# Output projections of a two-layer backbone on one Trainium2 core: each weight tile loaded and split for every chunk of columns, or once

## The chip, the cores and the metric

One core of a Trainium2 chip runs the whole program in one launch. The metric is device time in microseconds, the median of several executions; lower is better. All data are float32 in memory.

## The reference, cut to what matters

```python
# layer 0: two mixers side by side, one output projection (1024 -> 1024), for 256 context and 1024 latent tokens
y = jnp.concatenate([y_a, y_b], axis=-1) @ w_out       # ab_mixer: y_a gMLP half, y_b gated DeltaNet half
lat = lat + g1 * y_lat;  cx = cx + cg1 * y_ctx
lat = lat + g2 * conv_ffn(modulate(rms_norm(lat, norm2_g), sh2, sc2), w_up, conv_w, w_down)   # cx alike

# layer 1: latent attention, 8 heads of 128, 1024 latent tokens only
y_lat = block_attention(qn_l, qr_l, kn, kr, v) @ w_out  # (1024, 1024) @ (1024, 1024)
lat = lat + g1 * y_lat
lat = lat + g2 * conv_ffn(modulate(rms_norm(lat, norm2_g), sh2, sc2), w_up, conv_w, w_down)
```

## The kernel before

Activations lie in SBUF with features on the 128 partitions and tokens along the free side. `xa` holds the residual stream: 8 tiles of 128 features by 1280 tokens in layer 0 (256 context tokens first), by 1024 tokens in layer 1.

Every float32 product is made of three matmuls. `split` writes a float32 tile as two tiles of TensorE's fp32r type, a high part (a cast, L126 on POOL or L124 on ACT) and a low part (the difference, L133, on DVE; on POOL too where the engine is called "pools"). `mm3` then gives, for each tile of 128 input features, high x high (L140), high weight x low activation (L141) and low weight x high activation (L142). `weights` (L144) loads a raw weight tile `wur` through SP's DMA queue and splits it into `wuh` and `wul`; `stream` hands out such tiles by number, made on first use. The pool has 3 buffers for the raw tile and 2 each for the parts.

**Layer 0's second half.** The projection's input has two halves of 512 features. The second (`ybh`, `ybl`, from the DeltaNet scan's `o`) comes last. It is done in three chunks of tokens: 512 to 1023 (512 columns), 256 to 511 and 1024 to 1279 (256 columns each). For each chunk, `out0` (L1474) runs over 8 output tiles `ot`, each with 4 weight tiles of 128 x 128 in one 256 KB load, 12 matmuls, and one addition into `xa` on DVE (L1488). Since the chunks are the outer loop, the stream has 24 loads and 24 splits (of 128 x 512 each). Woven into the chunks are the RMS norms of the chunks before (sums `nsum`, `nall` on PE; `nm`, L229, L230 and six L266 on DVE with L264, L267 on ACT and L263 on POOL for the scaling) and the first operands of the ConvFFN, `B11` and `B21` (high part on POOL or ACT, low part on DVE). The scan's end stands directly ahead: `gdn_out` normalises the last two token tiles of `o` (L1468 to L1472; temporaries `osq`, `osr`, `osm`, `osg`), after which the last `ybh`, `ybl` are split.

**Layer 1.** `out1` (L1768) takes the attention output `o`, splits it into `oh` (ACT) and `ol` (DVE), and does three chunks of 512, 256 and 256 tokens (`END`) over 8 output tiles each, with 8 weight tiles of 128 x 128 in one 512 KB load, 24 matmuls and one addition (L1800). That makes 24 loads and 24 splits of 128 x 1024; the first three are "pools". The norms of the chunks before stand between them as in layer 0.

Behind each of the two stages comes the ConvFFN, whose first matmuls are `upa` (L408 to L410) on `B11`.

A framework with tile pools and a scheduler sets the order on each engine; every engine then works its list in order, and SP issues all loads and stores in one list. PSUM has 8 banks, 7 of them under one tag (`bank`, L118) for accumulators. Pool `hc` (and in layer 1 its counterpart) has "rooms", pairs of 128 x 2048 tiles that the ConvFFN's operands take: `room("B11", ...)` and so on. SBUF that a pool takes over from one that was released is guarded by the last users of the old tiles.

Of the kernel before, what the change touches and what calls it, by code (L numbers as in the profile page):

```python
# [7 lines left out]
F32 = mybir.dt.float32  # L8
# [7 lines left out]
P = 128  # L16
D = 1024
KD = D // P
# [17 lines left out]
END = [(0, 512), (512, 256), (768, 256)]  # L36
# [31 lines left out]
def weave(main, fill, n=1, rest=True):  # L68

    for _ in main:  # L70
        for _ in range(n):
            next(fill, None)
    if rest:
        drain(fill)
# [23 lines left out]
class Kern:  # L98
# [55 lines left out]
    def stream(self, pool, srcs, shape, tag, eng, bufs_raw=2, bufs=2, n=None):  # L154

        made = {}

        def get(i):
            if i not in made and i < len(srcs):
                made[i] = self.weights(pool, srcs[i], shape, tag, eng if isinstance(eng, str) else eng(i), bufs_raw, bufs, n)  # L160
            return made.get(i)
        return get
# [1605 lines left out]
    def out1(self, wp, op, o, xa, xd, g1, norm, ready):  # L1768


        nc, tc, I = self.nc, self.tc, self.I
        with ExitStack() as es:
            yp = es.enter_context(tc.tile_pool(name="y1", bufs=1))
            np_ = es.enter_context(tc.tile_pool(name="n2", bufs=1))
            get = self.stream(wp, [I["w_out1"][ot] for ot in range(KD)] * len(END), [P, KD, P], "wu",
                              lambda i: "pools" if i < 3 else "pool", 3)
            get(0)
            get(1)
            yh = yp.tile([P, KD, SEQ], F32R, name="oh")
# [9 lines left out]
            pend, i = iter(()), 0  # L1789
# [22 lines left out]
    def run(self):  # L1812
        nc, tc, I = self.nc, self.tc, self.I
        with ExitStack() as es:
# [54 lines left out]
            g1, sh2, gs2, g2 = self.modv(0, 2), self.modv(0, 3), self.gains(0, 4, ng[:, 1]), self.modv(0, 5)  # L1869
            xap = tc.alloc_tile_pool(name="xa", bufs=1)  # L1870
            xa = xap.tile([P, KD, NT], F32, name="xa")
            op = tc.alloc_tile_pool(name="yb", bufs=1)
            o = op.tile([P, NH, NC, P], F32, name="o")
# [26 lines left out]
            w_half1 = [I["w_out0"][1, ot] for ot in range(KD)]  # L1900
            next(scan)
            with ExitStack() as es2:
                yp = es2.enter_context(tc.tile_pool(name="y0a", bufs=1, side="right"))
                wp = es2.enter_context(tc.tile_pool(name="wo0a", bufs=2, side="right"))
                get = self.stream(wp, w_half1, [P, 4, P], "wo", "pool", 3)
                get(0)
                y = half1(yp, 0, CTX, 0)
# [5 lines left out]
            keep = lambda c0, cn: nc.sync.dma_start(dr["xs"][:, :, c0:c0 + cn], xa[:, :, c0:c0 + cn])  # L1913

            def norm(tmp, c0, cn, steps=True):
                r = 1 if c0 < CTX else 0
                return self.mod_x(tmp, [xv(k, c0, cn) for k in range(KD)], cn, gs2[:, r, :], sh2[:, r, :], steps)
            ffw = tc.alloc_tile_pool(name="ffw", bufs=2, side="right")
# [18 lines left out]
            with ExitStack() as es2:  # L1937
                yp = es2.enter_context(tc.tile_pool(name="y0b", bufs=1))
                np_ = es2.enter_context(tc.tile_pool(name="n0b", bufs=1))
                tmps = self.temps(np_, nsq=5, nr=1, nt=0, width=256)  # L1940
                get = self.stream(ffw, w_half1 * 3, [P, KD, P], "wu", "pool", 3, n=4)
                y = [half1(yp, 512, 512, 0), half1(yp, 256, 256, 1)]
                keep(0, CTX)
                weave(self.out0(get, [y[0]], xa, g1), norm(tmps, 0, CTX), 2)
                keep(512, 512)
                y.append(half1(yp, 1024, 256, 0))
                weave(self.out0(lambda i: get(KD + i), [y[1]], xa, g1), norm(tmps, 512, 256), 2)
                keep(256, 256)
                weave(self.out0(lambda i: get(2 * KD + i), [y[2]], xa, g1),
                      chain(norm(tmps, 768, 256), context(), firsts(), norm(tmps, 256, 256)), 3)  # L1950
                keep(1024, 256)
            op.release()
# [36 lines left out]
            h = {}  # L1989
# [207 lines left out]
```

## Time and profile before

| | us |
|---|---|
| median of 3 runs | 3290.85 (3288.29 to 3294.72) |
| profiled execution, whole | 3285.33 |
| its span in the profile | 3283.5 |
| PE busy | 3116.2 (95%) |
| DVE busy | 2180.9 (66%) |
| POOL busy | 1340.1 (41%) |
| ACT busy | 1105.7 (34%) |

The span is the time from the first to the last instruction of the core in the profiled execution. An engine's busy time is the sum over its instructions; the mean granted TensorE clock over the span was 0.978 of full speed. Times of single instructions are counted from the start of the span.

### The profile page before, as it was taken

The page shows a single profiled execution, that of the slowest core. Times are in us where ns is not written, and L with a number is a line of the kernel's source. Part 1 is how long each engine was busy: PE and PEld are TensorE (multiplying, and loading weights), DVE is VectorE, ACT ScalarE, POOL GpSimd, SP SyncE. Part 2 cuts the span into 40 slices and gives each one's busy share as a digit, 9 for nine tenths or more (in the row PEclk, how much of TensorE's full clock was granted, in tenths as well). Part 3 has the DMA queues.
Part 4 walks back from the last instruction along what each step waited for, and adds up shares of the span by engine and source line. Part 5 has one row for each costly group of instructions (what it writes and reads, how often), then busy time and mean ns, then how long its engine had stood idle before and what let it go on. Part 6 is the DMA issues. An engine that isn't in the chain of part 4 may idle for free. (4 is left out here: it accounts for less than half of the span.)

```text
span 3283.5 us, 48865 instructions
## 1 busy us (share of the span) xinstructions
PE 3116.2 (95%) x19029; PEld 2604.8 (79%) x19029; DVE 2180.9 (66%) x3245; ACT 1105.7 (34%) x2136; POOL 1340.1 (41%) x1210
## 2 busy tenths in 40 slices
PE   7999899998899999998999999999998899999998
PEld 5677777886677788886889778888987677778888
DVE  6332876567776678873487455666656788889355
ACT  5322233333333333340021245555542333333110
POOL 3234323654444354442355222222134566665243
PEclk9999999999899999999999999999999899999999
DMA  7344946753335421244457322000034122224554
GB/s 252 122 148 129 302 135 210 235 157 112 97 121 165 157 89 71 69 159 145 142 192 233 93 80 72 27 22 22 8 116 148 58 78 84 83 78 168 194 194 150
DMA packets 257959, 419.82 MB, mean 128 GB/s; under 512 B 47024, under 2 KB 163968, under 8 KB 257600
## 3 DMA queue, kind: packets, MB, share of 16 engines
q1 hardware_dynamic: 257728, 416.70, 39.6%
q8 instruction: 150, 2.46, 0.3%
q14 instruction: 81, 0.66, 0.1%
HBM read 335.85 MB, written 80.78 MB: 127 GB/s over the span
## 5 line engine op out<-in xcount | busy, mean ns | idle before, releaser
L632 PE MATMUL dn<-ah,wdh 128*128 128x256 f32 (+1 forms) x1232 | 391.1, 319 | 15.0 <-POOL wdh L126 12.9
L634 PE MATMUL dn<-ah,wdl 128*128 128x256 f32 (+1 forms) x1232 | 385.5, 319 | 11.2 <-DVE wdl L133 11.1
L633 PE MATMUL dn<-al,wdh 128*128 128x256 f32 (+1 forms) x1232 | 388.7, 317 | 0.0
L126 POOL TENSOR_SCALAR wdh<-wdr 128x1024 fp32r<-128x1024 f32 x154 | 192.1, 1249 | 345.7 <-PE dn L633 222.2
L133 DVE TENSOR_TENSOR wdl<-wdr,wdh 128x1024 fp32r<-128x1024 f32 x154 | 200.2, 1304 | 191.2 <-POOL wdh L126 187.6
L126 POOL TENSOR_SCALAR wuh<-wur 128x1024 fp32r<-128x1024 f32 (+1 forms) x142 | 171.0, 1205 | 270.1 <-PE upc L409 95.8
L632 PEld LDWEIGHTS dn<-ah,wdh 128*128 128x128 f32 x1232 | 237.4, 193 | 37.2 <-POOL wdh L126 13.9
L133 DVE TENSOR_TENSOR wul<-wur,wuh 128x1024 fp32r<-128x1024 f32 (+1 forms) x139 | 199.2, 1434 | 97.0 <-POOL wuh L126 96.6
L634 PEld LDWEIGHTS dn<-ah,wdl 128*128 128x128 f32 x1232 | 234.9, 193 | 30.3 <-DVE wdl L133 13.8
L633 PEld LDWEIGHTS dn<-al,wdh 128*128 128x128 f32 x1232 | 237.0, 192 | 15.3
L1719 POOL TENSOR_SCALAR p<-p,rsm 128x1280 f32<-128x1280 f32 x63 | 84.8, 1345 | 325.3 <-DVE rsm L1712 167.4
L674 DVE SCALAR_TENSOR_TENSOR y<-raw,fconv,y 128x1023 f32<-128x1023 f32 (+1 forms) x132 | 171.1, 1324 | 35.2 <-ACT y L420 34.9
L676 DVE SCALAR_TENSOR_TENSOR y<-raw,fconv,y 128x1023 f32<-128x1023 f32 (+1 forms) x132 | 187.6, 1443 | 0.1
L140 PE MATMUL proj<-hh,wih 128*128 128x512 f32 (+1 forms) x512 | 183.1, 359 | 0.0
L142 PE MATMUL proj<-hh,wil 128*128 128x512 f32 (+1 forms) x512 | 176.4, 345 | 1.0 <-DVE wil L133 1.0
L141 PE MATMUL proj<-hl,wih 128*128 128x512 f32 (+1 forms) x512 | 177.0, 346 | 0.1
L427 POOL TENSOR_TENSOR y<-y,y 128x1280 f32<-128x1280 f32 (+1 forms) x44 | 128.0, 2910 | 105.0 <-issue 58.4
L393 POOL TENSOR_TENSOR s<-wur 128x512 f32<-128x512 f32 x42 | 72.4, 1723 | 191.9 <-DMA wur<-in_w_up 140.8
L1701 DVE TENSOR_REDUCE mx<-sc 128x1 f32<-128x512 f32 (+1 forms) x192 | 114.6, 597 | 40.2 <-PE sc L1700 38.0
L420 ACT ACTIVATE y<-raw,fconv 128x1280 f32<-128x1280 f32 (+1 forms) x88 | 110.8, 1260 | 83.0 <-DVE raw L436 81.1
L111 ACT ACTIVATE p<-sc,nmx 128x512 f32<-128x512 f32 (+1 forms) x192 | 116.2, 617 | 49.1 <-DVE nmx L1705 48.9
L133 DVE TENSOR_TENSOR pl<-pt,ph 128x512 fp32r<-128x512 f32 (+1 forms) x192 | 108.8, 593 | 8.1 <-ACT ph L124 7.5
(535 smaller groups left out, 9268.2 us busy)
## 6 DMA issues: line engine op xcount, KB each, us to landing
wdr<-in_w_down SPq DMA_DIRECT2D x154, 512.0 KB, 3.8
adaw<-in_ada_w SPq DMA_DIRECT2D x96, 512.0 KB, 4.1
wur<-in_w_up SPq DMA_DIRECT2D x88, 512.0 KB, 3.6
al<-act SPq DMA_DIRECT2D x20, 1024.0 KB, 7.4
t<-t SPq DMA_DIRECT2D x20, 768.0 KB, 6.4
act<-y SPq DMA_DIRECT2D x22, 640.0 KB, 3.0
wur<-in_w_out SPq DMA_DIRECT2D x24, 512.0 KB, 3.5
act<-y SPq DMA_DIRECT2D x22, 512.0 KB, 2.6
```

The source lines that it names most:

```text
L111: self.nc.scalar.activation(out, in_, func, **kw)
L126: nc.gpsimd.tensor_scalar(dst, src, 1.0, 0.0, op0=ALU.mult, op1=ALU.add)
L133: (self.nc.gpsimd if eng == "pools" else self.nc.vector).tensor_tensor(lo, src, f(hi), ALU.subtract)
L140: nc.tensor.matmul(ps, wh, xh, start=first and i == 0, stop=False)
L141: nc.tensor.matmul(ps, wh, xl, start=False, stop=False)
L142: nc.tensor.matmul(ps, wl, xh, start=False, stop=last and i == n - 1)
L427: nc.gpsimd.tensor_tensor(y[1], y[0], y[1], ALU.mult)
L632: nc.tensor.matmul(pss[o], wh[:, q, :], ah, start=pr == j == 0, stop=False)
L633: nc.tensor.matmul(pss[o], wh[:, q, :], al, start=False, stop=False)
L634: nc.tensor.matmul(pss[o], wl[:, q, :], ah, start=False, stop=pr == npr - 1 and j == 1)
L674: nc.vector.scalar_tensor_tensor(out=y[:, s0 + 1:e], in0=raw[:, s0:e - 1], scalar=w[:, 0:1], in1=y[:, s0 + 1:e], op0=ALU.mult, op1=ALU.add)
L676: nc.vector.scalar_tensor_tensor(out=y[:, s0:e - 1], in0=raw[:, s0 + 1:e], scalar=w[:, 2:3], in1=y[:, s0:e - 1], op0=ALU.mult, op1=ALU.add)
```

## The change

In layer 0, the eight weight tiles of the second half are loaded as four pairs of 512 KB, each split once, into the rooms `T1` (pairs 0 and 1) and `B22` (pairs 2 and 3); all three chunks read them there. 24 loads and splits of 128 x 512 become 4 of 128 x 1024. In layer 1, output tiles 0 to 3 are loaded and split once, "pools" (high and low part on POOL), into rooms `B11` and `B21`; tiles 4 to 7 are streamed for each chunk as before, and the kept tiles 0 and 1 of the later chunks ask for tiles 4 and 5 ahead of time. 24 loads and splits become 16. In each layer the kept parts are called `wkh` and `wkl`; their rooms are taken by the ConvFFN's operands afterwards.

```diff
@@ out1
-            get = self.stream(wp, [I["w_out1"][ot] for ot in range(KD)] * len(END), [P, KD, P], "wu",
-                              lambda i: "pools" if i < 3 else "pool", 3)
+            keep = [t for r in ("B11", "B21") for t in zip(*[(h[:, 0:2], h[:, 2:4]) for h in self.room(r, "wk")])]
+            keep = [[t.rearrange("p a (b f) -> p (a b) f", f=P) for t in hl] for hl in keep]
+            srcs = [I["w_out1"][ot] for ot in range(4, KD)] * len(END)
+            stream = self.stream(wp, srcs, [P, KD, P], "wu", "pool", 3, 2)
+            made = set()
+
+            def get(i):
+                c, ot = divmod(i, KD)
+                if c == len(END):
+                    return None
+                if ot >= 4:
+                    return stream(4 * c + ot - 4)
+                if c == 0 and ot not in made:
+                    made.add(ot)
+                    raw = wp.tile([P, KD, P], F32, tag="wur", name="wur", bufs=3)
+                    nc.sync.dma_start(raw, I["w_out1"][ot])
+                    self.split(*keep[ot], raw, "pools")
+                if c and ot < 2:
+                    stream(4 * c + ot)
+                return keep[ot]
             get(0)
             get(1)
@@ run
-                get = self.stream(ffw, w_half1 * 3, [P, KD, P], "wu", "pool", 3, n=4)
+                made = {}
+
+                def get(i):
+
+                    i = i % KD
+                    if i // 2 not in made:
+                        j = i // 2
+                        raw = ffw.tile([P, KD, P], F32, tag="wur", name="wur", bufs=3)
+                        nc.sync.dma_start(raw.rearrange("p (o k) f -> p o k f", o=2),
+                                          I["w_out0"][1, 2 * j:2 * j + 2].rearrange("o p k f -> p o k f"))
+                        if j % 2 == 0:
+                            made["room"] = [t.rearrange("p a (b f) -> p (a b) f", f=P) for t in self.room(("T1", "B22")[j // 2], "wk")]
+                        made[j] = [t[:, 8 * (j % 2):8 * (j % 2) + 8] for t in made["room"]]
+                        self.split(*made[j], raw, "pool")
+                    return tuple(t[:, 4 * (i % 2):4 * (i % 2) + 4] for t in made[i // 2])
                 y = [half1(yp, 512, 512, 0), half1(yp, 256, 256, 1)]
                 keep(0, CTX)
                 weave(self.out0(get, [y[0]], xa, g1), norm(tmps, 0, CTX), 2)
                 keep(512, 512)
                 y.append(half1(yp, 1024, 256, 0))
-                weave(self.out0(lambda i: get(KD + i), [y[1]], xa, g1), norm(tmps, 512, 256), 2)
+                weave(self.out0(get, [y[1]], xa, g1), norm(tmps, 512, 256), 2)
                 keep(256, 256)
-                weave(self.out0(lambda i: get(2 * KD + i), [y[2]], xa, g1),
+                weave(self.out0(get, [y[2]], xa, g1),
                       chain(norm(tmps, 768, 256), context(), firsts(), norm(tmps, 256, 256)), 3)
```

What this does to the lists of the engines is to be seen in three places.

The first is POOL at the end of layer 0's scan. Before (`o<-o,osg` are the scan's last two products, `wuh` the weights' casts):

```order
L126 TENSOR_SCALAR wuh_7390<-wur_7388 128x512
L126 TENSOR_SCALAR wuh_7409<-wur_7407 128x512
L1472 TENSOR_TENSOR o_4541<-o_4541,osg_7162 128x4x128
L126 TENSOR_SCALAR wuh_7434<-wur_7432 128x512
L1472 TENSOR_TENSOR o_4541<-o_4541,osg_7166 128x4x128
L126 TENSOR_SCALAR wuh_7458<-wur_7456 128x512
L206 TENSOR_TENSOR nsq_7469<-xa_4537 128x256
L126 TENSOR_SCALAR wuh_7486<-wur_7484 128x512
```

And with the change (`wkh_7390` is room T1, `wkh_7472` room B22):

```order
L1472 TENSOR_TENSOR o_4541<-o_4541,osg_7162 128x4x128
L1472 TENSOR_TENSOR o_4541<-o_4541,osg_7166 128x4x128
L126 TENSOR_SCALAR wkh_7390<-wur_7388 128x1024
L126 TENSOR_SCALAR wkh_7390<-wur_7426 128x1024
L126 TENSOR_SCALAR wkh_7472<-wur_7470 128x1024
L206 TENSOR_TENSOR nsq_7455<-xa_4537 128x256
L126 TENSOR_SCALAR wkh_7472<-wur_7541 128x1024
```

The first cast of the projection's weights now stands behind the scan's last product, since room T1 lies where the scan's temporaries lay; four casts of 128 x 1024 are all there are, and the list goes on with the ConvFFN's weights.

The second is DVE at the same place. Before (L229 to L1471 are the scan's last normalisation; `wul` the weights' low parts):

```order
L1471 TENSOR_TENSOR o_4541<-o_4541,osr_7323 128x4x128
L133 TENSOR_TENSOR wul_7391<-wur_7388,wuh_7390 128x512
L133 TENSOR_TENSOR wul_7410<-wur_7407,wuh_7409 128x512
L229 SCALAR_TENSOR_TENSOR osq_7165<-osq_7165,osm_7336 128x512
L230 SCALAR_TENSOR_TENSOR osr_7335<-osq_7165,osr_7335 128x512
L1471 TENSOR_TENSOR o_4541<-o_4541,osr_7335 128x4x128
L1488 SCALAR_TENSOR_TENSOR xa_4537<-wo_7394,mv02_4526,xa_4537 128x512
L133 TENSOR_TENSOR wul_7435<-wur_7432,wuh_7434 128x512
```

And with the change:

```order
L229 SCALAR_TENSOR_TENSOR osq_7165<-osq_7165,osm_7336 128x512
L230 SCALAR_TENSOR_TENSOR osr_7335<-osq_7165,osr_7335 128x512
L1471 TENSOR_TENSOR o_4541<-o_4541,osr_7335 128x4x128
L133 TENSOR_TENSOR ybl256_7378<-o_4541,ybh256_7377 128x256 x3
L133 TENSOR_TENSOR wkl_7391<-wur_7388,wkh_7390 128x1024
L133 TENSOR_TENSOR ybl256_7378<-o_4541,ybh256_7377 128x256
L133 TENSOR_TENSOR wkl_7391<-wur_7426,wkh_7390 128x1024
L133 TENSOR_TENSOR wkl_7473<-wur_7470,wkh_7472 128x1024
L133 TENSOR_TENSOR wkl_7473<-wur_7541,wkh_7472 128x1024
L133 TENSOR_TENSOR wul_8004<-wur_7999,wuh_8003 128x1024
L1488 SCALAR_TENSOR_TENSOR xa_4537<-wo_7394,mv02_4526,xa_4537 128x512
```

The two low parts that stood inside the scan's last normalisation are gone; the first `wkl` stands behind it and behind three low parts of `ybl256`. All four `wkl`, and the first low part for the ConvFFN (`wul_8004`), stand ahead of the first addition L1488. On PE, the L140 and L141 of three output tiles now stand ahead of the first L142, where those of two did.

The third is POOL at the end of layer 1's attention. Before (`p` is the last softmax product):

```order
L126 TENSOR_SCALAR wuh_22776<-wur_22774 128x1024
L1717 TENSOR_SCALAR p_22640<-p_22640,rsm_22645 128x256
L133 TENSOR_TENSOR wul_22777<-wur_22774,wuh_22776 128x1024
L126 TENSOR_SCALAR wuh_22782<-wur_22780 128x1024
L133 TENSOR_TENSOR wul_22783<-wur_22780,wuh_22782 128x1024
L126 TENSOR_SCALAR wuh_22899<-wur_22897 128x1024
L133 TENSOR_TENSOR wul_22900<-wur_22897,wuh_22899 128x1024
```

And with the change (`wkh_22650` is room B11, `wkh_22652` room B21):

```order
L1717 TENSOR_SCALAR p_22516<-p_22516,rsm_22521 128x256
L126 TENSOR_SCALAR wkh_22650<-wur_22654 128x1024
L126 TENSOR_SCALAR wkh_22650<-wur_22658 128x1024
L126 TENSOR_SCALAR wkh_22652<-wur_22773 128x1024
L133 TENSOR_TENSOR wkl_22651<-wur_22654,wkh_22650 128x1024
L133 TENSOR_TENSOR wkl_22651<-wur_22658,wkh_22650 128x1024
L133 TENSOR_TENSOR wkl_22653<-wur_22773,wkh_22652 128x1024
L126 TENSOR_SCALAR wkh_22652<-wur_22803 128x1024
L133 TENSOR_TENSOR wkl_22653<-wur_22803,wkh_22652 128x1024
```

The first cast stood ahead of the last softmax product and now stands behind it; each low part followed its cast, and now three casts go ahead of the first low part, and four low parts instead of three are POOL's. Room B11 is also guarded by PE's last attention matmul (L142), which read what lay there. Here too the L140 and L141 of three output tiles now stand ahead of PE's first L142, instead of two L140 and one L141.

## Rows read from the trace of the kernel before

**Rows 1.** The page, costliest groups of instructions: splits into hi and lo.
```profile
L126 POOL TENSOR_SCALAR wuh<-wur 128x1024 fp32r<-128x1024 f32 (+1 forms) x142 | 171.0, 1205 | 270.1 <-PE upc L409 95.8
...
L133 DVE TENSOR_TENSOR wul<-wur,wuh 128x1024 fp32r<-128x1024 f32 (+1 forms) x139 | 199.2, 1434 | 97.0 <-POOL wuh L126 96.6
```

**Rows 2.** Waits of PE, 745 to 870 us: total us, times, longest us.
```profile
PE wo L140 <- POOL wuh L126: 8.2, 9, 3.9
PE wo L142 <- DVE wul L133: 5.9, 4, 2.4
```

**Rows 3.** Waits of PE, 2420 to 2570 us.
```profile
PE wo L142 <- DVE wul L133: 5.6, 2, 3.9
PE wo L140 <- POOL wuh L126: 4.6, 4, 1.5
PE wo L142 <- POOL wul L133: 1.7, 1, 1.7
```

**Rows 4.** Windows: length, PE, PEld, DVE, ACT, POOL busy (xcount), PEclk, DMA share, GB/s.
```profile
766.00:775.00 9.00, 5.08 (x17) 3.68 (x16) 7.57 (x10) 3.12 (x5) 3.34 (x3) 0.81 0.76 243
775.00:785.00 10.00, 10.00 (x50) 6.84 (x50) 6.96 (x11) 2.06 (x6) 4.22 (x5) 1.00 0.27 80
812.00:824.00 12.00, 7.31 (x50) 6.49 (x50) 10.14 (x19) 7.25 (x16) 6.47 (x7) 0.95 0.30 87
824.00:844.00 20.00, 16.23 (x117) 12.80 (x117) 17.45 (x27) 8.81 (x20) 10.78 (x13) 0.93 0.56 170
2497.00:2512.00 15.00, 8.76 (x63) 7.72 (x62) 15.00 (x14) 8.67 (x13) 11.16 (x7) 0.78 0.29 94
2530.00:2545.00 15.00, 11.84 (x84) 11.38 (x83) 12.32 (x16) 3.91 (x9) 5.09 (x6) 0.89 0.34 107
2560.00:2620.00 60.00, 44.82 (x227) 37.51 (x226) 45.37 (x45) 18.86 (x28) 28.46 (x17) 0.86 0.12 36
```

**Rows 5.** PE timeline, layer 0: start us, duration us, instruction, idle before.
```profile
766.25 0.28 PE L142 MATMUL wo<-ybh,wol 128*128 128x256 f32 x1
770.45 0.51 PE L140 MATMUL wo<-ybh,wuh 128*128 128x512 f32 x1 [3.92 <-POOL wuh L126]
...
771.63 0.73 PE L142 MATMUL wo<-ybh,wul 128*128 128x512 f32 x1
...
846.82 0.99 PE L408 MATMUL upa<-B11h,wuh 128*128 128x512 f32 x1
```

**Rows 6.** POOL timeline, layer 0.
```profile
769.32 1.66 POOL L126 TENSOR_SCALAR wuh<-wur 128x512 fp32r<-128x512 f32 x2 [6.78 <-DMA wur<-in_w_out]
...
776.14 1.29 POOL L1472 TENSOR_TENSOR o<-o,osg 128x512 f32<-128x512 f32 x1
```

**Rows 7.** ACT timeline, layer 0.
```profile
770.75 0.63 ACT L228 ACTIVATE osq<-osr 128x512 f32<-128x512 f32 x1
```

**Rows 8.** DVE timeline, layer 0.
```profile
770.43 2.78 DVE L133 TENSOR_TENSOR wul<-wur,wuh 128x512 fp32r<-128x512 f32 x2 [0.51 <-POOL wuh L126]
773.13 0.68 DVE L229 SCALAR_TENSOR_TENSOR osq<-osq,osm 128x512 f32<-128x512 f32 x1
...
779.67 1.50 DVE L133 TENSOR_TENSOR ybl<-o,ybh 128x256 fp32r<-128x256 f32 x3
...
835.48 5.69 DVE L266 SCALAR_TENSOR_TENSOR xa<-xa,gs,nr 128x256 f32<-128x256 f32 x6
```

**Rows 9.** POOL timeline, layer 1.
```profile
2420.00 1.05 POOL L126 TENSOR_SCALAR wuh<-wur 128x1024 fp32r<-128x1024 f32 x1 [2.65 <-ACT ph L124]
...
2421.47 2.39 POOL L133 TENSOR_TENSOR wul<-wur,wuh 128x1024 fp32r<-128x1024 f32 x1
```

**Rows 10.** PE timeline, layer 1.
```profile
2427.29 0.73 PE L140 MATMUL wo<-oh,wuh 128*128 128x512 f32 x2 [0.99 <-ACT oh L124]
...
2428.35 0.40 PE L142 MATMUL wo<-oh,wul 128*128 128x512 f32 x1
```

**Rows 11.** DVE timeline, layer 1.
```profile
2498.36 9.26 DVE L266 SCALAR_TENSOR_TENSOR xa<-xa,gs,t 128x512 f32<-128x512 f32 x6
```

## The prediction

> **What bounds the kernel now.** I began with the shares of busy time: PE 95%, everything else at 66% or less. So the kernel is TensorE's, and a change to two short stages can only be worth what PE loses in them. The chain that ended last says the same in its shares and gives no place; I therefore went to the waits of PE over each of the two stages.
>
> In layer 0's stage PE waited 8.2 us for high parts of the projection's weights, in 9 waits of which the longest took 3.9, and 5.9 us for low parts, in 4 waits [rows 2]. In layer 1's stage it waited 5.6 us for low parts from DVE, 4.6 for high parts, and 1.7 for one low part that POOL made [rows 3]. Together 26.0 us out of 3283.5. The reader should see that these are all waits on splits of weights, that is, on the work which the change cuts from 24 to 4 and from 24 to 16 splits.
>
> Then the windows, to see what else goes with the waits. Over 766 to 775 us PE was busy 5.1 of 9 us and the granted clock was 0.81; 775 to 785 is full and at full clock, 50 instructions in 10 us; in 812 to 844 PE was busy 7.3 of 12 and 16.2 of 20 us at 0.95 and 0.93 of full clock; in layer 1 the bad stretches are 2497 to 2512 (8.8 of 15 us, clock 0.78) and 2530 to 2545 (11.8 of 15, 0.89) [rows 4]. [...]
>
> Last, the timelines at both starts, because the lists of the engines show that the first split moves there.
>
> **Layer 0, what is removed.** All waits but the first: 8.2 - 3.9 + 5.9 = 10.2 us. After the first chunk all weights are there, so no cast can be late. The 20 splits that go took some 0.8 us each on POOL [rows 6] and up to 1.4 on DVE [rows 8]; neither engine's own time is on the path, apart from the waits counted. The clock: a granted 0.95 over 12 us and 0.93 over 20 us is half speed for 2 x 0.05 x 12 + 2 x 0.07 x 20 = 4.0 us, in which half the work is undone: 2.0 us back. The loads cost nothing either way: over 775 to 785 the DMA engines were busy 0.27 of the time [rows 4].
>
> **Layer 0, what is moved: a late start.** PE's last matmul of the stage before is at 766.25, and the first one on the new weights at 770.45, with the first L142 at 771.63 [rows 5]. POOL made the first two casts at 769.32, ahead of the scan's last product at 776.14 [rows 6]. With the change the cast stands behind that product. How early can the product come? ACT's L228 before it ended at 770.75 + 0.63 = 771.4 [rows 7]. DVE then has L229, L230 and L1471; L229 ran at 773.13 since two low parts took DVE from 770.43 for 2.78 us [rows 8], and these are gone. So three operations of 0.7 us from 771.4: 773.5. The product, 1.29 us [rows 6]: 774.8. The cast of 128 x 1024, 1.2 us on average [rows 1]: 776.0, and the first L140 at 776.1. The first low part stands on DVE behind three `ybl` (1.50 us [rows 8]), which need ACT's cast of the product and end at about 776.8; then 1.43 us [rows 1]: the first L142 at 778.3, which is 6.7 us later than at 771.63. In that hole PE does what it did later before: two more matmuls of 512 columns and some five sums of the norm, 1.5 us. Net loss 5.2 us. Bounds: 3 us if the product follows faster and DVE takes the low part first, 8 if the cast and low part take the time that they take beside another busy engine (the two low parts of half the size took 1.4 us each at 770.43).
>
> Layer 0 in sum: 10.2 + 2.0 - 5.2 = 7.0 us.
>
> **Layer 0, what is late next.** The stage's end is the first `upa` at 846.82 [rows 5], and it needs `B11`, whose low part comes after six L266 of 5.69 us at 835.48 on DVE [rows 8]. DVE loses 20 of 24 low parts, and this norm can start earlier as the chunk before it ends earlier; I let it move with the chunk, and put the case where it doesn't among the rivals.
>
> **Layer 1, what is removed.** The 1.7 us wait falls on an output tile that is now kept, and its low part is made some 5 us before PE comes to it. Of the other 10.2 us, half of the splits in the second and third chunk stay (8 of 16). A kept tile between two streamed ones gives the streams twice the time, so I expect more than half back; but the 3.9 us wait is for a low part which stands on DVE behind six L266 of 512 columns, 9.26 us at 2498.36 [rows 11], and those stay. I take two thirds: 6.8 us (bounds 3 and 10.2). The clock: half speed for 2 x 0.22 x 15 + 2 x 0.11 x 15 = 9.9 us, 5.0 us of work; two thirds of that is 3.3.
>
> **Layer 1, what is moved.** POOL made the first high part at 2420.00 and its low part at 2421.47 (2.39 us) [rows 9], during the attention. In the new order the first cast waits for PE's last attention matmul, since room B11 lies where that reads. PE sat 0.99 us ahead of 2427.29 [rows 10], so that matmul ended at 2426.3. Three casts of 1.05 us and one low part of 2.39: 2431.9. PE's first L142 comes at 2432.0 instead of 2428.35 [rows 10], 3.65 us late; three more matmuls of 0.23 us are done in the hole. Net loss 3.0 us. From there POOL makes a low part every 2.4 us, while PE needs 5.5 us for the 24 matmuls of one output tile, so it isn't overtaken again. Bounds: 1 and 6 us.
>
> Layer 1 in sum: 1.7 + 6.8 + 3.3 - 3.0 = 8.8 us.
>
> [...] After the 3.9 us wait at 770.45 PE ran at a granted 0.81 until 775, which is half speed for 2 x 0.19 x 9 = 3.4 us and 1.7 us of work [rows 4, 5]. [...] In layer 0 that stretch is in the time of before already. [...]
>
> **The rest.** [...]
>
> Sum: 7.0 + 8.8 + 2.0 = 17.8, say 18 us. Against the profiled execution's 3285.33 that gives 3267; the median of the runs is 5.5 us above that execution, so the forecast is 3290.85 - 18 = 3273 us.
>
> **Rivals.**
>
> A, the forecast: both stages gain as summed, 12 to 24 us. For it speaks that the waits are named and that the order shows them gone.
>
> B, the norms set the pace: six L266 of 5.69 and 9.26 us on DVE [rows 8, 11], with the low part of B11 behind, end as late as before apart from a few us, and PE waits for `nsum`, `npt` or B11 instead of weights. Then each layer keeps some 4 us: 8, 3283 us. DVE had only 2.5 of 20 us free in 824 to 844 [rows 4], which speaks for it; against it, eight or nine low parts were in that stretch, and these go.
>
> C, more: all of layer 1's 10.2 and 5.0 us come back and the hole of layer 0 is half as long: 18 + 5 + 2.6, about 26 us, 3265 us.
>
> D, the other side: on DVE the first addition L1488 stands behind the ConvFFN's first low part, and that behind its load. A raw buffer comes free for this load when the second `wkl` is done, at about 780; with load, cast and low part the addition follows at about 787. PE can fill six accumulators (the norm holds one of seven) of 12 matmuls, 2.8 us each, so it stops at about 795. There are 8 us to spare; the change loses only if that load lands 26 us later than I think, and by over 0.2% from 33 us on. Nothing in a DMA share of 0.27 at that time speaks for it; but loads stand in one list behind stores of `xa`, and I haven't seen it run.
>
> E, it is given back: behind layer 1's stage PE was busy 44.8 of 60 us, at clock 0.86 [rows 4]. If what it waits for there, and behind layer 0's stage, doesn't come earlier, the gain becomes a longer wait there: 3291 us. Against it: these waits hang on the norm of the last chunk, which moves with the stage.
>
> **Chances and numbers.** A 0.55, B 0.20, C 0.10, E 0.08, D 0.07. A change of under 0.2%, 6.6 us, can't be told from none here. Faster by more than that: A, C and three quarters of B, 0.80; within: the rest of B and E, 0.13; slower: D, 0.07. The range of 8 in 10, from C's 3265 less the error of its bounds to the worst end of B: 3260 to 3286.
>
> **What would show it.** In the changed kernel's profile: the first L142 on kept weights about 6.7 us after 771.63 and about 3.7 us after 2428.35; no waits of PE for weights in layer 0 behind the first; at most 4 us of them in layer 1's later chunks; full clock in the last chunk of layer 0; the first `upa` at about 839 in layer 0, and layer 1's 9 us before its old place relative to that. Wrong would make it: a first L142 after 785 in layer 0, additions later than 795, or a new wait of PE for B11 as long as the ones that went.

## The result and the profile after

| | before | changed |
|---|---|---|
| median, us | 3291.55 (4 runs, 3288.29 to 3294.72) | 3270.93 (4 runs, 3268.68 to 3274.09) |
| profiled execution, us | 3285.33 | 3269.30 |
| its span, us | 3283.5 | 3267.2 |
| PE, DVE, POOL, ACT busy, us | 3116.2, 2180.9, 1340.1, 1105.7 | 3102.1, 2166.1, 1321.0, 1103.7 |

The ratio of the times is 0.9944, with a 95% interval from 0.9932 to 0.9956: 20.6 us less by the medians, 16.3 by the two spans. The forecast was 3273 us and 18 us less.

The waits of PE in layer 0's stage, to be held against [rows 2]:

```profile
PE wo L140 <- POOL wkh L126: 9.6, 1, 9.6
PE nall L217 <- DVE npt L214: 2.8, 4, 1.0
...
PE nsum L196 <- POOL nsq L206: 0.7, 1, 0.7
```

And in layer 1's, against [rows 3]:

```profile
PE wo L140 <- POOL wkh L126: 2.4, 3, 1.3
PE wo L142 <- DVE wul L133: 2.3, 2, 1.5
PE wo L142 <- POOL wkl L133: 1.5, 1, 1.5
...
PE upa L408 <- POOL wuh L126: 0.9, 1, 0.9
PE wo L141 <- DVE ol L133: 0.8, 1, 0.8
```

In layer 0 one wait for the projection's new weights is left, the first, and it grew from 3.9 to 9.6 us. The wait for the norm's sums, which DVE copies (`npt`) before PE's `nall` can read them, grew from 0.6 to 2.8 us. In layer 1, the 11.9 us for weights of the projection became 6.2, of which 3.9 (`wkh`, `wkl`) are at the start; `upa` and `ol` are new with 1.7 us.

The windows (length, busy time and instructions of PE, PEld, DVE, ACT and POOL, granted clock, DMA share, GB/s) of the same two stages, against [rows 4]:

```profile
775.00:780.00 5.00, 2.80 (x6) 1.82 (x6) 3.51 (x4) 1.33 (x4) 4.41 (x4) 0.50 0.40 148
...
785.00:805.00 20.00, 19.39 (x89) 15.07 (x88) 13.58 (x21) 6.05 (x15) 6.04 (x6) 1.00 0.37 123
805.00:824.00 19.00, 18.38 (x158) 16.54 (x156) 14.53 (x28) 10.73 (x27) 4.73 (x6) 1.00 0.30 111
824.00:839.00 15.00, 12.68 (x91) 9.35 (x90) 12.47 (x21) 8.67 (x19) 4.33 (x5) 1.00 0.28 97
...
2418.00:2444.00 26.00, 21.24 (x80) 15.68 (x79) 24.25 (x26) 9.61 (x26) 18.25 (x10) 0.87 0.71 243
...
2485.00:2505.00 20.00, 19.13 (x158) 17.91 (x158) 15.31 (x17) 9.00 (x15) 8.42 (x7) 1.00 0.12 34
2505.00:2521.00 16.00, 16.00 (x132) 14.86 (x130) 12.90 (x18) 3.57 (x6) 5.66 (x5) 1.00 0.51 158
2521.00:2537.00 16.00, 13.61 (x80) 10.48 (x79) 15.45 (x16) 7.58 (x15) 10.81 (x9) 1.00 0.60 193
```

From 785 us to the end of layer 0's stage the clock is full, where it was 0.93 to 0.95 from 812 to 844; in layer 1 the place of the 0.78 and the 0.89 is at full clock too. At both starts a stretch runs at half clock. In layer 0 that is not new: the 0.50 over 775 to 780 stands in the place of the 0.81 over 766 to 775 [rows 4]. In layer 1 it is: 0.87 on average over 2418 to 2444, with 0.50 in each us from 2423 to 2429, where the same window of before, with the stage's start in it, has 1.00:

```profile
2418.00:2444.00 26.00, 21.55 (x113) 17.20 (x112) 17.05 (x36) 15.38 (x39) 12.01 (x8) 1.00 0.77 273
```

PE's rows of layer 0, against [rows 5]: the last matmul of the stage before, the first two of the new weights, the change to 256 columns, and `upa`:

```profile
767.36 0.28 PE L142 MATMUL wo<-ybh,wol 128*128 128x256 f32 x1
777.20 0.79 PE L140 MATMUL wo<-ybh,wkh 128*128 128x512 f32 x1 [9.56 <-POOL wkh L126]
...
782.23 0.50 PE L142 MATMUL wo<-ybh,wkl 128*128 128x512 f32 x1
...
804.74 0.28 PE L140 MATMUL wo<-ybh,wkh 128*128 128x256 f32 x1
...
838.71 0.58 PE L408 MATMUL upa<-B11h,wuh 128*128 128x512 f32 x1
```

Layer 1's start, against [rows 10], the last attention matmul, the first two on the kept weights:

```profile
2418.39 0.28 PE L142 MATMUL o<-ph,vl 128*128 128x256 f32 x1
2419.92 0.50 PE L140 MATMUL wo<-oh,wkh 128*128 128x512 f32 x1 [1.25 <-POOL wkh L126]
...
2425.57 0.79 PE L142 MATMUL wo<-oh,wkl 128*128 128x512 f32 x1 [1.54 <-POOL wkl L133]
```

The length of each stage is the better measure, since the code outside them, which is the same, took up to 7 us more in one profile than in another. Layer 0's stage, from the last `woh` matmul to the first `upa`, took 80.6 us before (766.25 to 846.82 [rows 5]) and takes 71.4 (767.36 to 838.71). Layer 1's, from the last attention matmul to the first ConvFFN matmul on `T1`, took 136.5 us and takes 128.2 (2418.39 to 2546.63).

### The profile page after: what moved, and what is told of

It reads as the page before. It is cut to its first block, busy times and chain, and to the rows that moved or that the text cites. A ratio compares the mean times of both kernels' runs of the same rounds, so it can differ in the third digit from the quotient of the medians.

```text
span 3267.2 us, 48692 instructions
## 1 busy us (share of the span) xinstructions
PE 3102.1 (95%) x19029; PEld 2595.6 (79%) x19029; DVE 2166.1 (66%) x3216; ACT 1103.7 (34%) x2136; POOL 1321.0 (40%) x1183
## 5 line engine op out<-in xcount | busy, mean ns | idle before, releaser
L634 PEld LDWEIGHTS dn<-ah,wdl 128*128 128x128 f32 x1232 | 231.9, 190 | 31.5 <-DVE wdl L133 15.1
L133 DVE TENSOR_TENSOR wul<-wur,wuh 128x1024 fp32r<-128x1024 f32 x106 | 167.1, 1577 | 97.8 <-POOL wuh L126 97.7
L126 POOL TENSOR_SCALAR wuh<-wur 128x1024 fp32r<-128x1024 f32 x106 | 135.1, 1276 | 203.4 <-PE upc L409 94.9
L674 DVE SCALAR_TENSOR_TENSOR y<-raw,fconv,y 128x1023 f32<-128x1023 f32 (+1 forms) x132 | 169.6, 1313 | 35.3 <-ACT y L420 34.9
L140 PE MATMUL proj<-hh,wih 128*128 128x512 f32 (+1 forms) x512 | 185.0, 363 | 0.0
L676 DVE SCALAR_TENSOR_TENSOR y<-raw,fconv,y 128x1023 f32<-128x1023 f32 (+1 forms) x132 | 181.8, 1399 | 0.1
L142 PE MATMUL proj<-hh,wil 128*128 128x512 f32 (+1 forms) x512 | 177.8, 348 | 1.3 <-DVE wil L133 1.3
L141 PE MATMUL proj<-hl,wih 128*128 128x512 f32 (+1 forms) x512 | 178.5, 349 | 0.3 <-DVE hl L254 0.2
L393 POOL TENSOR_TENSOR s<-wur 128x512 f32<-128x512 f32 x42 | 78.5, 1869 | 194.5 <-DMA wur<-in_w_up 129.6
L140 PEld LDWEIGHTS proj<-hh,wih 128*128 128x128 f32 x512 | 98.3, 193 | 20.5 <-issue 8.0
```

The lines of the kernel that those rows point to most:

```text
L126: nc.gpsimd.tensor_scalar(dst, src, 1.0, 0.0, op0=ALU.mult, op1=ALU.add)
L133: (self.nc.gpsimd if eng == "pools" else self.nc.vector).tensor_tensor(lo, src, f(hi), ALU.subtract)
L140: nc.tensor.matmul(ps, wh, xh, start=first and i == 0, stop=False)
L141: nc.tensor.matmul(ps, wh, xl, start=False, stop=False)
L142: nc.tensor.matmul(ps, wl, xh, start=False, stop=last and i == n - 1)
L634: nc.tensor.matmul(pss[o], wl[:, q, :], ah, start=False, stop=pr == npr - 1 and j == 1)
```

## The experiments

Theory: the gain is the waits for split weights and the clock that they cost, less a late start in each layer; so a stage without the late start is shorter still. Rivals: the norm chain on DVE sets the pace and the start costs nothing; the depth of the buffers did it, not the number of splits; the two parts hang together.

The stages of all kernels, from the profiles (differences of starts, to 0.1 us; layer 0 counted here from the last L140 on `woh`, 0.2 us ahead of the last matmul), and the times:

| kernel | layer 0: first L142 after the stage before, us | stage, us | layer 1: first L142 after the attention, us | stage, us | median, us | ratio to before (95%) |
|---|---|---|---|---|---|---|
| before | 5.6 | 80.8 | 2.3 | 136.5 | 3291.55 (4) | 1 |
| changed | 15.1 | 71.6 | 7.2 | 128.2 | 3270.93 (4) | 0.9944 (0.9932 to 0.9956) |
| after_again | 16.1 | 72.6 | 7.2 | 128.3 | 3267.73 (5) | 0.9942 (0.9930 to 0.9955) |
| l0_only | 16.1 | 72.6 | 2.3 | 138.6 | 3280.20 (11) | 0.9977 (0.9968 to 0.9985) |
| l0_only_again | 16.1 | 72.6 | 2.3 | 138.8 | 3282.50 (11) | 0.9984 (0.9975 to 0.9993) |
| l1_only | 6.3 | 82.8 | 7.2 | 129.4 | 3282.30 (12) | 0.9985 (0.9975 to 0.9994) |
| l1_only_again | 6.1 | 80.9 | 7.2 | 128.3 | 3282.63 (11) | 0.9985 (0.9976 to 0.9993) |
| l0_start | 8.4 | 74.9 | 7.2 | 128.3 | 3276.84 (5) | 0.9969 (0.9957 to 0.9980) |
| l0_resplit | 15.0 | 83.9 | 7.2 | 128.3 | 3285.78 (11) | 0.9989 (0.9980 to 0.9997) |
| l0_ring | 6.1 | 68.3 | 7.2 | 129.6 | 3266.46 (5) | 0.9937 (0.9924 to 0.9951) |
| l1_start | 15.0 | 71.5 | 3.8 | 127.0 | 3268.26 (5) | 0.9948 (0.9936 to 0.9960) |
| l1_dve | 16.1 | 72.6 | 4.0 | 124.0 | 3265.81 (5) | 0.9936 (0.9923 to 0.9949) |
| best_a | 6.3 | 68.7 | 4.0 | 123.7 | 3263.62 (5) | 0.9933 (0.9920 to 0.9947) |
| best_b | 6.3 | 68.8 | 2.3 | 123.0 | 3263.89 (5) | 0.9927 (0.9914 to 0.9939) |

The number of runs stands in brackets. The kernels below the second row were measured in three groups, each with before beside it on one chip: l0_only, l1_only, l0_start and l1_start with before at 3287.1 us (23 runs); after_again, l0_ring, l0_resplit and l1_dve at 3287.98 (15); best_a, best_b, l0_only_again and l1_only_again at 3287.72 (21).

**One part alone.** l0_only has the changed loop in `run` and the old `get` in `out1`, l1_only the reverse:

```diff
 l0_only:
-            keep = [t for r in ("B11", "B21") for t in zip(*[(h[:, 0:2], h[:, 2:4]) for h in self.room(r, "wk")])]
...
+            get = self.stream(wp, [I["w_out1"][ot] for ot in range(KD)] * len(END), [P, KD, P], "wu",
+                              lambda i: "pools" if i < 3 else "pool", 3)
 l1_only:
-                made = {}
-
-                def get(i):
...
+                get = self.stream(ffw, w_half1 * 3, [P, KD, P], "wu", "pool", 3, n=4)
```

> Layer 0's part alone, layer 1 as before. If the two parts add up as in the prediction's sum (layer 0: 7.0 us and 1 us of refills), this is 8 to 10 us faster than before, about 3282 us, and in the profile the first upa of layer 0 stands near 838.7 us as in the changed kernel. If the gain of layer 0 is given back in its ConvFFN (rival E), under 3 us faster.

> Layer 1's part alone, layer 0 as before. The sum says 8.8 us and 1 us of refills: 8 to 11 us faster than before, about 3282 us. If the two parts hang together (a changed DMA list in layer 0 shifting layer 1, say), the two single gains differ from the 20.6 us of both by more than 4 us.

By its own stage each part is what the sum said: layer 0 gains 8.2 us (80.8 to 72.6), layer 1 between 7 and 8 (136.5 to 129.4, and to 128.3). By the medians they came to 6.9 and 4.8 us, 11.7 together against the whole's 20. So I measured them and the whole again.

> The changed kernel once more, beside the three below on one chip, as the measure for them. Its gain over before should be 15 to 22 us, if the first comparison holds and if the single parts (6.9 and 4.8 us) were only loosely measured; if the parts really add up to less than the whole, it stays near 20 while the parts stay at 12.

> Layer 0's part alone, measured a second time, since the two single gains (6.9 and 4.8 us) fell short of the whole's 20 us. If the parts add up, as the lengths of the two stages say (8 to 9 us each), one of the two comes out larger now and the sum is 15 to 20. If they don't, the sum stays near 12, and something outside the two stages gains from having both.

> Layer 1's part alone, measured a second time, for the same reason. Adding up: 7 to 10 us faster than before. Not adding up: 4 to 6 us again.

The whole: 20.3 us. The parts: 5.2 and 5.1 us. So the medians of the parts don't add up to that of the whole, 8 to 10 us are short, and this holds in the second measurement. About half of it is in the table: the stage that a part leaves alone came out longer than in before's profile, layer 1's 138.6 and 138.8 us in l0_only instead of 136.5, layer 0's 82.8 in l1_only, 80.9 in the repeat, instead of 80.8. Both stages together are 6.2 and 6.0 us shorter than before's in l0_only, 5.1 and 8.2 in l1_only, 17.5 and 16.5 in the changed kernel. Before has a single profile here, so whether its own stages were short in that one execution is not shown. Outside the two stages the profiles of all kernels range over 7 us for the same code (3064.8 to 3071.5), most of it ahead of layer 0's stage; l1_only's two profiles, of one kernel, have 3071.0 and 3065.9. What makes up the other half stays open.

**The late start of layer 0.** l0_start makes the first pair twice: in a streaming buffer for the first chunk, in the room for the others.

```diff
+                def get0(i):
+                    if i == 6:
+                        get(0)
+                    if i >= 2:
+                        return get(i)
+                    if not pair0:
+                        raw = ffw.tile([P, KD, P], F32, tag="wur", name="wur", bufs=3)
...
+                        pair0.extend(ffw.tile([P, KD, P], F32R, tag="wu" + p, name="wu" + p, bufs=2) for p in "hl")
+                        self.split(*pair0, raw, "pool")
+                    return tuple(t[:, 4 * i:4 * i + 4] for t in pair0)
-                weave(self.out0(get, [y[0]], xa, g1), norm(tmps, 0, CTX), 2)
+                weave(self.out0(get0, [y[0]], xa, g1), norm(tmps, 0, CTX), 2)
```

> The changed kernel, but the first pair of layer 0 is split into a streaming buffer for the first chunk (as before the change, ahead of the scan's last product) and split again into its room later: one load and one split more. Theory (the late start is a real loss): the first L142 comes near 773 us instead of 782.2, and 5 to 9 us come back against the changed kernel, about 3264 us. Rival (the norm chain paces the stage, the hole at the start costs nothing): first L142 early, but upa where it was, same time as the changed kernel, 3271 us.

The first L142 did come 6.7 us earlier, and the stage got 2 to 3 us longer: neither case of the expectation. DVE's rows of l0_start in the middle of the first chunk:

```profile
791.73 1.23 DVE L133 TENSOR_TENSOR wul<-wur,wuh 128x1024 fp32r<-128x1024 f32 x1 [1.56 <-POOL wuh L126]
...
793.89 1.23 DVE L133 TENSOR_TENSOR wul<-wur,wuh 128x1024 fp32r<-128x1024 f32 x1 [0.28 <-POOL wuh L126]
...
795.70 0.41 DVE L214 COPY npt<-nsum 128x256 f32<-128x256 f32 x1
797.42 0.42 DVE L219 TENSOR_SCALAR nm<-nall 128x256 f32<-128x256 f32 x1 [1.31 <-PE nall L217]
```

And PE's at that place, and two windows around it:

```profile
796.16 1.22 PE L217 MATMUL nall<-npt,cst 128*128 128x256 f32 x2 [3.95 <-DVE npt L214]
```

```profile
785.00:796.00 11.00, 7.21 (x35) 5.18 (x33) 8.41 (x10) 0.00 (x0) 3.74 (x3) 0.98 0.80 228
796.00:801.00 5.00, 4.84 (x11) 3.81 (x12) 0.96 (x3) 2.17 (x6) 0.61 (x1) 0.50 0.43 125
```

DVE does the ConvFFN's two low parts (`wul`) at 791.73 and 793.89, as soon as their loads and casts are there, and only then, at 795.70, the copy `npt` for which PE's `nall` stands waiting, 3.95 us. PE's list goes no further until then, and the five us behind run at a granted 0.50. The prediction's rival D is this queue: low parts for the ConvFFN, behind a load, ahead of what the projection needs. In the changed kernel it just misses, since PE is later itself and the second `wul` stands at 791.06: the load and the split that l0_start does twice are part of the delay. Whether the early start is worth anything without that queue is what the next kernel tells.

**The same without the queue.** l0_ring leaves pairs 0 and 1 in the two streaming buffers for all chunks, so that the ConvFFN's weights can't be split before the last chunk is through with them; pairs 2 and 3 share room T1, and the first pair comes in two loads and two splits.

```diff
-                        if j % 2 == 0:
...
-                        made[j] = [t[:, 8 * (j % 2):8 * (j % 2) + 8] for t in made["room"]]
+                        if j < 2:
+                            made[j] = [ffw.tile([P, KD, P], F32R, tag="wu" + p, name="wu" + p, bufs=2) for p in "hl"]
+                        else:
+                            if j == 2:
+                                made["room"] = [t.rearrange("p a (b f) -> p (a b) f", f=P) for t in self.room("T1", "wk")]
+                            made[j] = [t[:, 8 * (j - 2):8 * (j - 2) + 8] for t in made["room"]]
```

> The changed kernel, but layer 0's pairs 0 and 1 are split into the two streaming buffers and stay there for all three chunks (the first pair in two loads and two splits), and only pairs 2 and 3 go into a room, T1. No split is doubled, the first cast doesn't wait for the scan, and the ConvFFN's first low parts can't be hoisted ahead of the additions. Theory (the late start is a loss of its own, and it was the hoisted low parts that took it back in the last experiment): first L142 some 6 us after the last matmul of the stage before instead of 15, no wait for npt over 1 us, stage 5 to 9 us shorter than the changed kernel's 71.6, time 5 to 8 us less than the changed kernel. Rival (the norm chain alone sets the stage's end): stage within 2 us of 71.6.

```profile
PE nall L217 <- DVE npt L214: 3.9, 3, 2.4
PE wo L140 <- POOL wuh L126: 3.9, 1, 3.9
```

The first wait is 3.9 us again, as before the change, and the stage is 68.3 us, 3 to 4 shorter than the changed kernel's, where the theory had 5 to 9. The late start was a loss, but of the 9 to 10 us by which the first L142 is earlier, the stage keeps less than half. The first chunk ends 6.2 us earlier against the stage's start than in the changed kernel (7.2 than in its repeat); from there to `upa` it takes 36.9 us instead of 34.0, since `npt` waits, of which the longest is 2.4 us, come in the last chunks, where the ConvFFN's low parts now are. By the median it is 1.3 us less than the changed kernel beside it, inside the intervals; the stage's length is the evidence.

**Number or depth.** l0_resplit has the changed kernel's rooms, eight tiles deep, but loads and splits for each chunk.

```diff
-                    i = i % KD
-                    if i // 2 not in made:
-                        j = i // 2
+                    if i // 2 not in made and i < 3 * KD:
+                        j = i // 2 % 4
```

> The changed kernel, but in layer 0 every chunk loads and splits its pairs again into the same places of the two rooms: 12 loads of 512 KB and 12 splits of 128 x 1024 instead of 4, with eight output tiles of depth instead of two. Tells the number of splits from the depth of their buffers. Theory of the prediction (the number of splits is what costs: DVE and POOL are too full in the norm's stretches): half or more of layer 0's gain of 8 to 9 us goes, about 5 us slower than the changed kernel. Rival (before, PE waited only because a split could not be made more than one tile ahead): within 2 us of the changed kernel.

The whole gain of layer 0 is gone: stage 83.9 us, 3285.78 us, 18 slower than the changed kernel beside it, where about 5 were expected. Its waits of PE:

```profile
PE nall L217 <- DVE npt L214: 10.0, 4, 4.4
PE wo L140 <- POOL wkh L126: 9.6, 1, 9.6
```

No wait for weights at all behind the first, and 10.0 us for `npt` instead:

```profile
805.00:821.00 16.00, 11.99 (x91) 10.21 (x90) 15.69 (x23) 7.46 (x16) 6.16 (x6) 1.00 0.70 231
```

Over these 16 us, in which PE waits 4.0 us for `npt`, DVE is busy 15.7: the eight more low parts stand on DVE, and what stands behind them is late. The depth does remove the waits that the prediction counted, and it buys little. l0_resplit has the changed kernel's late start; from the end of the first chunk to `upa` it takes 46.4 us, before 49.1 and the changed kernel 34.0. So of the 15.1 us there, by these stretches, some 2.6 came with the depth (and with splits of twice the size), and 12.5 with the number of splits. Of the 18 us, the stage has 11; the rest is elsewhere, as with the parts.

**The start of layer 1.** l1_start starts the first chunk on two streamed tiles:

```diff
+            order = [(4, 5, 0, 1, 2, 3, 6, 7), range(KD), range(KD)]
-            stream = self.stream(wp, srcs, [P, KD, P], "wu", "pool", 3, 2)
+            stream = self.stream(wp, srcs, [P, KD, P], "wu", lambda i: "pools" if i < 2 else "pool", 3, 2)
```

> The changed kernel, but layer 1's first chunk does the output tiles in the order 4, 5, 0, 1, 2, 3, 6, 7, so that it starts on two streamed tiles whose splits don't wait for the attention's last matmul. Theory: the first L142 follows the last attention matmul by 2.3 us as before instead of 7.2, and 3 to 5 us come back, about 3267 us. Rival: the low parts on DVE and the POOL subtractions now fall together and the kept tiles come late: no gain, 3271 us.

The first L142 came 3.8 us after the attention instead of 7.2 (2.3 were expected), but the stage is only 1.2 us shorter, 127.0: nearer the rival. In its place came

```profile
PE wo L141 <- DVE ol L133: 1.7, 1, 1.7
```

where the changed kernel waits 0.8 us for `ol`. l1_dve leaves the order and gives the kept low parts to DVE:

```diff
-                    self.split(*keep[ot], raw, "pools")
+                    self.split(*keep[ot], raw, "pool")
```

> The changed kernel, but in layer 1 the kept tiles' low parts are made by DVE instead of POOL. Theory (POOL's three subtractions at the start, 2.8 us each, make the first L142 late and slow DVE's ol, 0.95 us each instead of 0.44): first L142 some 4 us after the last attention matmul instead of 7.2, ol back at about 0.45 us, stage 2 to 4 us shorter. Rival (DVE has 24 ol to make there and the low parts stand between them): ol ends later, the wait moves to L141, no gain.

The first L142 comes 4.0 us after the attention, and the stage is 124.0 us, 4.2 shorter: the theory's case, just above its 2 to 4. What POOL's subtractions did there is plain from the view of tile `ol` (count, shortest, median and longest duration in ns, first and last start). The changed kernel:

```profile
L133 DVE TENSOR_TENSOR ol<-o,oh x24: 406/552/2871, 2419.6 to 2442.7; 128x256 fp32r<-128x256 f32 x16, 128x512 fp32r<-128x512 f32 x8
```

l1_dve, with POOL doing casts alone:

```profile
L133 DVE TENSOR_TENSOR ol<-o,oh x24: 415/419/1518, 2418.2 to 2433.4; 128x256 fp32r<-128x256 f32 x16, 128x512 fp32r<-128x512 f32 x8
```

and the two rows of POOL in the changed kernel, to be held against [rows 9]:

```profile
2418.82 3.93 POOL L126 TENSOR_SCALAR wkh<-wur 128x1024 fp32r<-128x1024 f32 x3 [5.97 <-PE o L142]
2422.72 8.37 POOL L133 TENSOR_TENSOR wkl<-wur,wkh 128x1024 fp32r<-128x1024 f32 x3
```

Three subtractions took 2.79 us each where one took 2.39, and an `ol` beside them took up to 2.87 us, where the longest in l1_dve took 1.52.

**Both.** best_a is l0_ring and l1_dve together, best_b has l1_start's order too.

> The two edits that shortened a stage, together: layer 0 with pairs 0 and 1 in the streaming buffers, layer 1 with the kept tiles' low parts on DVE. The stages were 3.5 and 4.3 us shorter than the changed kernel's; if they add up, 7 to 8 us less than the changed kernel's 3267.7, near 3260 us, 0.9915 of before. If the second stage's gain is given back in its ConvFFN, 3264 us.

> As best_a, and layer 1's first chunk starts on the two streamed tiles (order 4, 5, 0, 1, 2, 3, 6, 7). If the hole at layer 1's start still costs (first L142 4.0 us after the last attention matmul where 2.3 is possible), 1 to 2 us less than best_a, 3259 us. Rival: DVE has the kept low parts and 24 ol in the same stretch, and is the bound there: same as best_a or a little more.

The stages add up: 68.7 and 123.7 us in best_a, 7.4 us less than the changed kernel's 71.6 and 128.2 and 8.5 less than in its repeat; best_b has 68.8 and 123.0, with its first L142 2.3 us after the attention, as before the change. The times are 3263.62 and 3263.89 us, 24 us less than before beside them, where the changed kernel had 20 in its own group: the expectation's other case, 3264, by the time. The stages kept their gain, though, and it isn't given back behind layer 1: from the first ConvFFN matmul on `T1` to the end best_a takes 722.4 us, the changed kernel 720.5 and 722.1. The last step, from best_a to best_b, is 0.6 us in the stage and nothing in the median. Whether either beats the changed kernel is not told apart by the intervals (0.9933 and 0.9927 against 0.9942, each to about 0.0013).

## Why the prediction was right, step by step

**Layer 0's waits and clock.** As predicted: no wait for weights behind the first, full clock in the last chunk. These two terms, 10.2 and 2.0 us, and half of the sum's 2.0 us, an estimate of mine for refills of PE behind the waits, were to give 13.2 us. One more row of before gives the end of the first chunk there, the first matmul of 256 columns:

```profile
797.77 0.28 PE L140 MATMUL wo<-ybh,wuh 128*128 128x256 f32 x1
```

From it to `upa` [rows 5] took 49.1 us before and takes 34.0 (804.74 to 838.71): 15.1 us, 2 more than forecast. The windows of these two stretches show where:

```profile
797.70:846.80 49.10, 37.34 (x247) 28.64 (x247) 41.84 (x67) 20.82 (x47) 24.21 (x28) 0.93 0.55 174
804.70:838.70 34.00, 31.05 (x247) 25.88 (x246) 26.77 (x48) 19.70 (x45) 9.05 (x11) 1.00 0.28 102
```

PE's idle time fell by 8.8 us (11.8 to 2.9) and not by 10.2, mainly since its waits for `npt` grew here from 0.6 to 2.2. Its busy time for the same 247 instructions fell by 6.3 us. Counted as in the prediction, a clock of 0.93 over 49.1 us is 3.4 us of work, not 2.0; the half speed that this counts with is in the windows of single us of before, 1.00 in each from 812 to 822 and 0.50 in each from 823 to 826. The 2.9 left stand where the sum has the 1.0 for refills. No run shows a refill of PE; what the rows of before show in its place is that the matmul behind a wait was followed by the next 0.22 us later (798.52 and 798.74), where it was 0.12 in the same shape without a wait (799.46 and 799.58): up to 1.2 us for the 12 waits for weights in this stretch. The rest stays open. One thing had changed there that the sum doesn't have: the six L266 took 5.69 us [rows 8] and take 3.88, on a DVE beside which POOL has no weights to cast (busy 5.5 of 5.8 us there before, 2.8 of 3.9 now); what that alone is worth was not measured.

```profile
831.93 3.88 DVE L266 SCALAR_TENSOR_TENSOR xa<-xa,gs,nr 128x256 f32<-128x256 f32 x6
```

**Layer 0's late start.** The first L140 was to come 9.85 us after the last matmul ahead (776.1 against 766.25); it came 9.84 us after (777.20 against 767.36). The chain, L228, three DVE operations, the product, the cast, was right to the tenth. The first L142 was to come 2.2 us later and came 5.0 later: what was mis-sized are the DVE rows behind it.

```profile
773.98 0.69 DVE L1471 TENSOR_TENSOR o<-o,osr 128x512 f32<-128x512 f32 x1
776.49 3.27 DVE L133 TENSOR_TENSOR ybl<-o,ybh 128x256 fp32r<-128x256 f32 x3 [1.82 <-ACT ybh L124]
779.69 1.21 DVE L133 TENSOR_TENSOR wkl<-wur,wkh 128x1024 fp32r<-128x1024 f32 x1
...
790.03 0.75 DVE L1488 SCALAR_TENSOR_TENSOR xa<-wo,mv,xa 128x512 f32<-128x512 f32 x1
```

Three `ybl` were to take 1.50 us and took 3.27, beside POOL's casts, and the low part was done 1.5 us later than forecast. PE did not stand idle for it: it did eight matmuls and ten sums instead of six and five, and among its waits there is none for a low part. The loss is that of the first wait, 9.56 us instead of 3.92: the first chunk ended 5.9 us later against the start of the stage (804.74 - 767.36 = 37.4, before 797.77 - 766.25 = 31.5), where 5.2 were foreseen; 6.9 in the repeat. l0_ring says what the start was worth in the end: 3 to 4 us, less than 5.2, because the stage's end gives some back.

**Layer 0 in sum.** 7.0 us and a share of 1.0 of the refills were forecast; the stage is 9.2 us shorter by its rows, 8.2 in the repeat.

**Layer 1's waits and clock.** "At most 4 us" was said of the later chunks; they have 2.3 for `wul`, and `upa` has 0.9. Waits for a low part behind six L266 stayed, as foreseen, but the longest fell from 3.9 to 1.5 us. The clock came back entirely, not by two thirds.

**Layer 1's late start.** Forecast 3.65 us later for the first L142; it was 7.2 us after the attention instead of 2.3, 4.9 later. POOL's rows above are the cause: three casts took 1.31 us each, not 1.05, and the low part 2.79, not 2.39. I took both from [rows 9], where DVE did something else beside them (see the last section). The matmuls behind the hole ran at the lower clock, for which the sum has no term here, at a granted 0.50 from 2423 to 2429 and 1.00 again from 2430 on:

```profile
2426.16 0.63 PE L140 MATMUL wo<-oh,wkh 128*128 128x512 f32 x1
...
2429.56 0.39 PE L142 MATMUL wo<-oh,wkl 128*128 128x512 f32 x1
```

some nine of them at 0.43 us from start to start instead of 0.23, 1.8 us. With three more matmuls done in the hole (0.7 us) the start cost about 6 us by this sum, not 3.0. l1_dve got 4.2 of that back with one word.

**Layer 1 in sum.** 8.8 us and the other 1.0 of the refills were forecast; the stage is 8.3 us shorter than before's, 10.4 shorter than the unchanged one of l0_only. A larger loss and a larger gain than foreseen cancelled; that the sum came out so near is luck.

**The rivals.** E didn't happen. Behind layer 1's stage PE waits 8.4 us for `T1` before and after alike, and `T1` moved with the stage. Behind layer 0's, from the first `upa` to the last attention matmul, it took 1579.2 us before and takes 1579.7. B has a part: in l0_resplit the norm's copies on DVE are what PE waits for, and in l0_start they ate the early start. In the changed kernel it comes to some 2 us of `npt`, because the change takes away most of what stood ahead of them on DVE. D was real and near: the first addition stood at 790.03, not 787, and an earlier start of PE, with one more load and split, is enough to bring the stall, as l0_start shows.

## What to carry to other kernels

A wait names what came last; count what stands ahead of it on the engine that it waits for. l0_resplit took away every wait for weights behind the first and gained nothing, since the same DVE then was late with something else; taking the splits away took the time. A buffer borrowed from what comes later is also guarded by what lay there before: work out from which instruction on it may be written, and start on a buffer that is free. And work that moved to POOL was not free for DVE here: an `ol`, which reads two operands from SBUF, took 2.85 us beside POOL's subtraction and 0.68 beside an idle POOL.

## What the runs showed of the hardware

In layer 1 of the changed kernel POOL's subtractions and DVE's `ol`, which read two operands from SBUF, took longer beside one another. These are single instructions there, the last of them beside an idle POOL:

```profile
2422.72 2.79 POOL L133 TENSOR_TENSOR wkl<-wur,wkh 128x1024 fp32r<-128x1024 f32 x1
2423.21 2.85 DVE L133 TENSOR_TENSOR ol<-o,oh 128x512 fp32r<-128x512 f32 x1
2425.47 2.83 POOL L133 TENSOR_TENSOR wkl<-wur,wkh 128x1024 fp32r<-128x1024 f32 x1
2425.99 2.86 DVE L133 TENSOR_TENSOR ol<-o,oh 128x512 fp32r<-128x512 f32 x1
...
2431.56 0.68 DVE L133 TENSOR_TENSOR ol<-o,oh 128x512 fp32r<-128x512 f32 x1
```

Each of the first two `ol` starts beside one of POOL's subtractions and ends 0.55 us after it (2426.06 against 2425.51, 2428.85 against 2428.30): 0.68 us of work took 2.85. POOL's second subtraction ends 2.24 us after the `ol` that it started beside, 2.83 us in all instead of the 2.39 of [rows 9]. Beside POOL's casts, which have one input, it was the same with `ybl` (3.27 us for three instead of 1.50). With one of DVE's operands in PSUM it was not: before the change, the `pl` of the attention, of whose two operands PE wrote `pt` to PSUM, ran beside POOL's cast and subtraction of [rows 9] at 0.61 us each (the longest of 60 from 2300 us on took 0.69),

```profile
2420.05 2.45 DVE L133 TENSOR_TENSOR pl<-pt,ph 128x512 fp32r<-128x512 f32 x4
```

and that subtraction took 2.39 us, the next one, with DVE idle, 2.38.

The other is the spread of the rest: code that is the same in all kernels, outside the two stages, took up to 7 us more in one profile than in another, and 5 us more in one of two profiles of the same kernel (l1_only). A gain of 5 us in a stage is better seen in the stage's own rows than in the time of one execution.
